# Expert outputs stored one row per slot and summed at the end; all token rows gathered by DMA

## The chip, the cores and the metric

The kernel runs on one core of a Trainium2 chip. The metric is the time of one execution on the device in microseconds (us), the median of several runs. All data are float32; "f32r" in tile types is float32 in the form that TensorE takes at its faster rate.

## The reference

Two encoder layers work on 512 tokens of width 1024. Each layer has a token mixer (attention and spatial gating) and then a mixture of experts, and it is the second half that is changed:

```python
scores = jax.nn.sigmoid((xt @ router_w).astype(jnp.float32))
...                                   # group-limited choice of 8 of 64 experts per token
wts = wts / jnp.sum(wts, -1, keepdims=True) * ROUTED_SCALE
...
def run_block(args):
    e, toks, ws = args
    xb = x_pad[toks]
    hb = jax.nn.silu(xb @ w_gate[e]) * (xb @ w_up[e])
    return (hb @ w_down[e]) * ws[:, None]
...
routed = jax.ops.segment_sum(yb.reshape(P, D), tok_buf, num_segments=T + 1)[:T]
shared = (jax.nn.silu(xt @ ws_gate) * (xt @ ws_up)) @ ws_down
return (routed + shared).reshape(B, S, D)
...
x = layer_norm(ALPHA * x + gate2 * y, ln2_g[l], ln2_b[l])
```

So 512 x 8 = 4096 rows of expert output have to reach 512 rows of the result. Each expert has 3 MB of weights (gate, up, down), 64 experts per layer.

## The kernel before

The experts are ranked by their number of tokens, and rank r has a fixed capacity `CAPS[r]`; the capacities add up to 43 **units** of 128 slots per layer (`UNITS`), each of one expert or of parts of two to four. A loop over an overflow count (L1141) takes what does not fit. The loop over `u_` (L1231) runs one unit after another: `gate_up` (L768), `turn` (L781), `down` (L793), with `swiglu` and the transposed copy between them on ACT and DVE. Weights come on SyncE's queue through rings: `we` (gate and up halves, 6 buffers, and 2 more as `w2`) and `wd` (3 buffers); a load waits until its buffer is free, and SP issues in program order.

**Inputs of a unit.** Units go in pairs. `mark_pair` (DVE, L1018) writes a one-hot matrix P of token by slot. For most pairs, `gather` on TensorE multiplies P with the token rows, split in two parts `xH` and `xL` (L1034, L1035: 64 matmuls a pair), into PSUM, and ACT and DVE write the modulated `xg` (L1040, L1042). For 8 of the 22 pairs of a layer (`by_dma`: even pairs 4 to 18), `bring_pair` fetches the rows from a copy of x in DRAM (`xd`) by two indirect DMAs of GpSimd (L1116) one pair ahead, and TensorE only transposes them (L1031, 16 per pair). `slots` (L1049) gives each slot's weight and token index by matmuls with P; GpSimd copies the indices of a unit's later segments to partition 0 (L1075).

**Outputs of a unit.** `down` leaves 128 rows `y` on DVE (L800), times weight and gate. `scatter` (L1084) adds them to a DRAM buffer by indirect DMAs with an add in the DMA, one for each segment of the unit, in turn on two buffers `accd[0]` and `accd[1]`; empty slots go to dump rows. The buffers are cleared first, and the shared expert's rows are written to `accd[0]` (L809 to L830). GpSimd also scales x and adds the bias during the first units (`stream`, L1169).

**The end of a layer.** Once unit 40 is scattered, `collect` loads the two buffers (8 loads of 512 KB, L1201) and GpSimd and DVE add them to x (L1207, L1208). The last two units (`LATE`) are not scattered: their rows are split and multiplied back by a one-hot `PT` on TensorE (L1297). Then each of the four tiles of 128 tokens is summed (L1302) and normalised, in the second layer scaled with `lnr` (loaded at L1278 and L1279, behind `collect` on SP's queue) and stored (L1285 to L1287). DVE, GpSimd and SP take their instructions in program order.

## Time and profile before

| | |
|---|---|
| median of 3 runs | 2220.01 us (2219.6 to 2223.42) |
| profiled execution | 2219.3 us, of which 2217.5 us are the span |
| TensorE (PE) busy | 2082.7 us, 94% of the span |
| DVE, ACT, GpSimd (POOL) busy | 1000.0, 518.9, 517.9 us |
| moved by DMA | 604.92 MB, mean 273 GB/s |
| mean granted TensorE clock | 0.985 |

"Span" is the time from the first to the last instruction; some 2 us lie around it. The busy share of PE is that of pipelined instructions that overlap, so 94% does not say that it works at its peak. "DMA share" in a stretch is the mean busy share of the 16 DMA engines; it reads 1.02 where they are never idle.

### The profile page before, as it was taken

How to read it: one execution, taken by the hardware profiler on the slowest of the kernel's cores; microseconds unless marked ns; L12 is line 12 of the kernel's file. 1: busy time of each engine (PE TensorE's matmuls, PEld its weight loads, DVE VectorE, ACT ScalarE, POOL GpSimd, SP SyncE). 2: the span in 40 equal slices, each digit the busy share in tenths (PEclk: the TensorE clock that was granted, in tenths of full speed). 3: DMA queues.
4: the chain of work that ended last, by engine and by line, in shares of the span. 5: the costliest groups of instructions: out<-in, count | busy, mean ns of one | idle time of the engine just before them, and what ended most of it. 6: DMA issues, size and time to landing. Idle time of an engine off the chain costs nothing. (4 is left out here: it accounts for less than half of the span.)

```text
span 2217.5 us, 31205 instructions
## 1 busy us (share of the span) xinstructions
PE 2082.7 (94%) x12088; PEld 1242.8 (56%) x12088; DVE 1000.0 (45%) x1920; ACT 518.9 (23%) x1005; POOL 517.9 (23%) x499
## 2 busy tenths in 40 slices
PE   5999999999999999999898999999999999999994
PEld 4888887464444444435477888855544435344442
DVE  6777866442222232222587675653422222222226
ACT  3463232211111111111144633222111111111111
POOL 3101002224222122212371000022522212222214
PEclk9999999999999999999999999999999999999997
DMA  7503755558999999999644045636799999999984
GB/s 271 187 29 126 243 211 191 232 201 300 383 382 384 392 383 385 382 384 348 221 140 139 11 150 163 205 114 247 275 328 380 385 390 383 381 363 384 391 291 156
DMA packets 113495, 604.92 MB, mean 273 GB/s; under 512 B 13984, under 2 KB 13984, under 8 KB 63424
## 3 DMA queue, kind: packets, MB, share of 16 engines
q1 hardware_dynamic: 90608, 525.82, 60.5%
q0 software_dynamic: 22736, 77.07, 14.1%
q8 instruction: 97, 1.59, 0.3%
q14 instruction: 54, 0.44, 0.1%
HBM read 542.54 MB, written 60.29 MB: 272 GB/s over the span
## 5 line engine op out<-in xcount | busy, mean ns | idle before, releaser
L768 PE MATMUL ps<-we,xg 128*32 128x512 f32 (+2 forms) x3648 | 642.6, 596 | 14.5 <-DMA we<-in_w_exp 10.4
L768 PEld LDWEIGHTS ps<-we,xg 128*32 128x32 f32 (+2 forms) x3648 | 198.2, 123 | 354.9 <-issue 316.5
L793 PE MATMUL ps<-wd,hTt 128*32 128x512 f32 (+2 forms) x1888 | 363.1, 595 | 19.6 <-DMA wd<-in_w_exp 16.1
L775 DVE TENSOR_TENSOR h<-h,ps 128x256 f32<-128x256 f32 x94 | 39.6, 421 | 556.8 <-ACT h L773 556.8
L1084 POOL DMA_INDIRECT accd<-y,ii x82 | 123.0, 1500 | 579.4 <-DVE y L800 476.4
L793 PEld LDWEIGHTS ps<-wd,hTt 128*32 128x32 f32 (+2 forms) x1888 | 118.5, 126 | 245.9 <-issue 195.7
L1034 PE MATMUL ps<-P,xH 128*128 128x256 f32 (+1 forms) x896 | 220.7, 286 | 6.0 <-DVE P L1018 6.0
L800 DVE SCALAR_TENSOR_TENSOR y<-ps,wc,r 128x512 f32<-128x512 f32 x172 | 128.9, 750 | 190.1 <-PE ps L793 190.1
L1035 PE MATMUL ps<-P,xL 128*128 128x256 f32 (+1 forms) x896 | 213.8, 282 | 0.0
L298 PE MATMUL ps<-wL,hH 128*128 128x512 f32 (+1 forms) x512 | 196.0, 383 | 7.3 <-DVE wL L294 7.3
L297 PE MATMUL ps<-wH,hH 128*128 128x512 f32 (+1 forms) x512 | 197.8, 386 | 4.2 <-ACT hH L193 4.2
L299 PE MATMUL ps<-wH,hL 128*128 128x512 f32 (+1 forms) x512 | 195.7, 382 | 0.0
L1034 PEld LDWEIGHTS ps<-P,xH 128*128 128x128 f32 x896 | 168.4, 188 | 19.3 <-issue 14.3
L1040 ACT ACTIVATE xg<-ps,f 128x256 f32<-128x256 f32 (+1 forms) x176 | 93.7, 559 | 356.9 <-DVE xg L1042 356.9
L1035 PEld LDWEIGHTS ps<-P,xL 128*128 128x128 f32 x896 | 168.5, 188 | 3.3 <-issue 3.3
L1042 DVE TENSOR_SCALAR xg<-ps,f 128x256 f32<-128x256 f32 (+1 forms) x176 | 90.5, 535 | 160.1 <-PE ps L1035 150.2
L193 ACT ACTIVATE hTt<-ps 128x256 f32<-128x256 f32 x94 | 36.1, 384 | 462.1 <-PE ps L781 462.1
L193 ACT ACTIVATE wH<-w 128x1024 fp32r<-128x1024 f32 x83 | 87.8, 1060 | 218.3 <-PE ps L299 129.5
L294 DVE TENSOR_TENSOR wL<-w,wH 128x1024 fp32r<-128x1024 f32 x84 | 109.9, 1310 | 54.2 <-ACT wH L193 54.0
L235 DVE SCALAR_TENSOR_TENSOR acc<-wa,cond,acc 128x1024 f32<-128x1024 f32 x80 | 117.1, 1464 | 12.8 <-issue 4.8
L298 PEld LDWEIGHTS ps<-wL,hH 128*128 128x128 f32 x512 | 98.8, 193 | 26.8 <-DVE wL L294 8.7
L297 PEld LDWEIGHTS ps<-wH,hH 128*128 128x128 f32 x512 | 98.5, 192 | 24.2 <-ACT hH L193 5.3
(326 smaller groups left out, 2566.3 us busy)
## 6 DMA issues: line engine op xcount, KB each, us to landing
we<-in_w_exp SPq DMA_DIRECT2D x256, 1024.0 KB, 16.7
wd<-in_w_exp SPq DMA_DIRECT2D x128, 1024.0 KB, 16.1
wa<-in_w_ada SPq DMA_DIRECT2D x96, 512.0 KB, 4.4
w<-in_wA SPq DMA_DIRECT2D x92, 512.0 KB, 4.3
sums<-accd SPq DMA_DIRECT2D x16, 512.0 KB, 7.1
accd<-zero POOLq DMA_DIRECT2D x12, 512.0 KB, 6.5
we<-in_w_sh SPq DMA_DIRECT2D x4, 1024.0 KB, 9.1
xd<-x SPq DMA_DIRECT2D x8, 512.0 KB, 2.6
```

Source lines behind the costliest of these rows:

```text
L193: return act.activation(out, in_, AF.Copy)
L235: dve.scalar_tensor_tensor(acc, w, cond[:, k:k + 1], acc, op0=OP.mult, op1=OP.add)
L294: dve.tensor_sub(l_out, src, h_out.bitcast(F32))
L297: pe.matmul(ps, aH, wH, start=first, stop=False)
L298: pe.matmul(ps, aH, wL, start=False, stop=False)
L299: pe.matmul(ps, aL, wH, start=False, stop=last)
L768: pe.matmul(ps[c:c + m, :], xT[:, k, c:c + m], ws[s][:, kk * 512:(kk + 1) * 512], start=k == 0, stop=k == NK - 1)
L793: pe.matmul(ps[c:c + m, :], t[:, j, c:c + m], ws[s][:, j * 1024 + nh * 512:j * 1024 + (nh + 1) * 512], start=j == 0, stop=j == 1)
L800: dve.scalar_tensor_tensor(y[0:n, hs], ps[0:n], wcol[0:n], gate2[0:n, hs], op0=OP.mult, op1=OP.mult)
L1034: pe.matmul(o, xH[:, i, k * 128:(k + 1) * 128], P[:, i, 0:n], start=i == 0, stop=False)
L1035: pe.matmul(o, xL[:, i, k * 128:(k + 1) * 128], P[:, i, 0:n], start=False, stop=i == NT - 1)
L1084: gp.indirect_dma_start(out=accd[turn_of[0]], out_offset=IndirectOffsetOnAxis(ap=ii[0:n, 0:1], axis=0), in_=y[col:col + n, :], in_offset=N ...
```

## The change

- A DRAM buffer `ysl` per layer has one row for each token and choice, 4096 rows. `slots` also computes the place of each slot (token x 8 + the number of earlier ranks that the token chose, from a small matmul with `above`), and `scatter` writes all 128 rows of a unit by one indirect DMA without an add. Slots without a token get an index past the bound and are skipped, in the gathers too.
- `collect` reads the 4096 rows back, 16 loads of 1 MB through the rings of `we` and `w2`. Per tile of 128 tokens DVE adds the first four rows, and TensorE the other four through `ident`. Units 41 and 42 stay `LATE`; zeros are scattered to their places when their rows are brought.
- All 22 pairs are brought by DMA, two pairs ahead, into four row buffers `rowbuf`, and transposed. `xH`, `xL`, the one-hot gather and GpSimd's index copies are gone.
- The shared expert's rows stay in SBUF (`ysh`, written by DVE) and GpSimd adds them to x in `stream`; `accd`, its clearing and the dump rows are gone.

```diff
-    accd = [dram.tile([640, D], F32, name=f"accd{a}") for a in range(2)]
-    xd = dram.tile([640, D], F32, name="xd")
+    xd = dram.tile([T, D], F32, name="xd")
+
+    ysl = [dram.tile([T * TOP, D], F32, name=f"ysl{l}") for l in range(DEPTH)]
...
-        xH = bp.tile([128, NT, D], F32R, name="xH")
+        ysh = bp.tile([128, NT, D], F32, name="ysh")
...
-                    acopy(y[0:n, hs], ps[0:n])
-                    gp.tensor_tensor(y[0:n, hs], y[0:n, hs], gate2[0:n, hs], op=OP.mult)
+                    dve.tensor_tensor(y[0:n, hs], ps[0:n], gate2[0:n, hs], op=OP.mult)
...
-        zero = bp.tile([128, D], F32, tag="y", bufs=3, name="zero")
-        gp.memset(zero, 0.0)
-        if l == 0:
-            gp.dma_start(xd[512:640, :], zero)
-        gp.dma_start(accd[0][512:640, :], zero)
-        for i in range(NT + 1):
-            gp.dma_start(accd[1][i * 128:(i + 1) * 128, :], zero)
...
         def shared_down(i):
-            y = down(sh_h[i], SH, 128, None)
-            gp.dma_start(accd[0][i * 128:(i + 1) * 128, :], y)
+            down(sh_h[i], SH, 128, None, ysh[:, i])
 
...
+        t1 = kc[:, C_T1:C_T1 + 4]
+        dve.tensor_scalar(WT[:, :, 192], t1, float(T + 1), float(TOP), op0=OP.subtract, op1=OP.mult)
+        dve.tensor_scalar(WT[:, :, 193], t1, float(T + 1), None, op0=OP.subtract)
+        dve.tensor_copy(WT[:, :, 194:196], t1[:, :, None].to_broadcast([128, NT, 2]))
...
-        xL = bring.tile([128, NT, D], F32R, tag="L16", name="xL")
-        for i in range(NT):
-            dve.tensor_sub(xL[:, i], x[:, i], xH[:, i].bitcast(F32))
...
+        def gather(rows, xg):
+
+            for k2 in range(4):
+                ps = psum()
+                for kk in range(2):
+                    for b_, r in enumerate(rows):
+                        pe.transpose(ps[:, kk * 256 + b_ * 128:kk * 256 + (b_ + 1) * 128],
+                                     r[:, (k2 * 2 + kk) * 128:(k2 * 2 + kk + 1) * 128], ident)
...
+        def slots(P, base, segs, rank, row):
+
+            ps = psum()
+            for i in range(NT):
+                pe.matmul(ps[:, 0:196], P[:, i, base:base + 128], WT[:, i], start=i == 0, stop=i == NT - 1)
+            sl = bp.tile([128, 196], F32, tag="sl", bufs=2, name="sl")
+            acopy(sl, ps[:, 0:196])
+            it = bp.tile([128, 1], I32, tag="it", bufs=4, name="it")
+            dve.tensor_scalar(it, sl[:, 193:194], float(T), None, op0=OP.add)
+            gp.indirect_dma_start(out=row, out_offset=None, in_=xd, in_offset=IndirectOffsetOnAxis(ap=it[:, 0:1], axis=0),
+                                  bounds_check=T - 1, oob_is_err=False)
+            wc = bp.tile([128, 1], F32, tag="wc", bufs=10, name="wc")
+            ii = bp.tile([128, 1], I32, tag="ii", bufs=10, name="ii")
+            tk = bp.tile([128, 1], F32, tag="tk", bufs=10, name="tk")
+            for r, off, col, n in segs:
+                for c, m in [(col, n)] if col == 0 else _pieces(col, n):
+                    b = slice(c, c + m)
+                    hi, lo, j = (sl[b, ds(rank + a, 1)] if rank is not None else sl[b, a + r:a + r + 1]
+                                 for a in (0, 64, 128))
+                    dve.tensor_tensor(wc[b], hi, lo, op=OP.add)
+                    dve.scalar_tensor_tensor(ii[b], j, float(T * TOP), sl[b, 192:193], op0=OP.add, op1=OP.add)
+            dve.tensor_copy(tk, sl[:, 194:195])
+            return wc, ii, tk
+
+        def scatter(y, ii):
+            gp.indirect_dma_start(out=ysl[l], out_offset=IndirectOffsetOnAxis(ap=ii[:, 0:1], axis=0), in_=y,
+                                  in_offset=None, bounds_check=T * TOP - 1, oob_is_err=False)
+
...
+        def mark_pair(p):
+            if not units_of(p):
+                return
+            P = bp.tile([128, NT, 256], F32R, tag="P", bufs=2, name="P")
+            for b_, u_ in enumerate(units_of(p)):
+                onehot(UNITS[u_], P, b_ * 128, lambda r: PW[:, :, r:r + 1])
+            Pd[p] = P
+
+        def bring_pair(p):
+
+            if not units_of(p):
+                return
+            P = Pd.pop(p)
+            for b_, u_ in enumerate(units_of(p)):
+                G[u_] = slots(P, b_ * 128, UNITS[u_], None, rowbuf[:, p % 2 * 2 + b_])
+                if u_ >= n_units - LATE:
+                    zero = bp.tile([128, D], F32, tag="y", bufs=3, name="zero")
+                    gp.memset(zero, 0.0)
+                    scatter(zero, G[u_][1])
+
+        def turn_pair(p):
+            xg = bp.tile([128, NK, 256], F32, tag="xg", bufs=2, name="xg")
+            gather([rowbuf[:, p % 2 * 2 + b_] for b_ in range(len(units_of(p)))], xg)
+            for b_, u_ in enumerate(units_of(p)):
+                G[u_] = xg[:, :, b_ * 128:(b_ + 1) * 128], *G[u_]
+
+        H = {}
+        mark_pair(0)
+        rowbuf = bring.tile([128, 4, D], F32, tag="L16", name="rowbuf")
+        bring_pair(0)
+        mark_pair(1)
+        bring_pair(1)
         shared_down(2)
         shared_turn(3)
...
 
 
...
                 gp.tensor_tensor(x[:, i], x[:, i], lnr[:, 1], op=OP.add)
                 yield
+                gp.tensor_tensor(x[:, i], x[:, i], ysh[:, i], op=OP.add)
+                yield
...
         def collect():
 
-            sums = []
             for i in range(NT):
-                t = bring.tile([128, 2, D], F32, tag="w", bufs=6, name="sums")
-                for a in range(2):
-                    nc.sync.dma_start(t[:, a], accd[a][i * 128:(i + 1) * 128, :])
-                sums.append(t)
-            for i, eng in ((0, gp), (2, gp), (1, dve), (3, dve)):
-                if eng is dve:
-                    yield
-                t = sums[i]
-                eng.tensor_tensor(t[:, 0], t[:, 0], t[:, 1], op=OP.add)
-                eng.tensor_tensor(x[:, i], x[:, i], t[:, 0], op=OP.add)
-            yield
...
+                for a in range(TOP // 2):
+                    t = wnew(0).rearrange("p (j d) -> p j d", j=2)
+                    src = ysl[l].rearrange("(t j) d -> t j d", j=TOP)
+                    nc.sync.dma_start(t, src[i * 128:(i + 1) * 128, 2 * a:2 * a + 2, :])
+                    got.append(t)
+
+        got = []
         for u_ in range(n_units + 1):
             if u_ % 2:
-                for p in (u_ // 2 + 2, u_ // 2 + 3):
-                    if by_dma(p) == (p == u_ // 2 + 3):
-                        mark_pair(p)
-            elif u_:
-                next_pair(u_ // 2 + 1)
-                if by_dma(u_ // 2 + 2):
-                    bring_pair(u_ // 2 + 2)
+                mark_pair(u_ // 2 + 3)
+            else:
+                if u_:
+                    turn_pair(u_ // 2 + 1) if units_of(u_ // 2 + 1) else None
+                bring_pair(u_ // 2 + 2)
...
-                slots_pair(*pair0)
-                next_pair(1)
+                turn_pair(1)
...
                 if u_ - 1 < n_units - LATE:
-                    scatter(y, UNITS[u_ - 1], idx)
+                    scatter(y, idx)
...
+                    collect()
                 drain(slow, 3)
...
+            mine = got[i * TOP // 2:(i + 1) * TOP // 2]
+            fin = [psum() for _ in range(2)]
...
-                                  start=own and n == 0 and a == 0, stop=n == LATE - 1 and a == 1)
-            if own:
-                for h in range(2):
-                    hs = slice(h * 512, (h + 1) * 512)
-                    dve.tensor_tensor(x[:, i, hs], fin[i, h], x[:, i, hs], op=OP.add)
-            normalise(x[:, i], [x[:, i, h * 512:(h + 1) * 512] if own else fin[i, h] for h in range(2)], 1e-5, True, both=i == NT - 1)
+                        pe.matmul(fin[h], PT[:, i * 128:(i + 1) * 128], yg[:, a, h * 512:(h + 1) * 512],
+                                  start=n == 0 and a == 0, stop=False)
+            for t in mine[:2]:
+                for j in range(2):
+                    dve.tensor_tensor(x[:, i], x[:, i], t[:, j], op=OP.add)
+            for n, t in enumerate(mine[2:]):
+                for j in range(2):
+                    for h in range(2):
+                        pe.matmul(fin[h], ident, t[:, j, h * 512:(h + 1) * 512], start=False, stop=n == 1 and j == 1)
```

## Rows read from the trace of the kernel before

**Rows 1.** Stretches of 40 us, first layer: span, PE, PEld, DVE, ACT, POOL, clock, DMA.

```profile
440.00:480.00 40.00, 37.07 (x218) 25.87 (x219) 11.88 (x35) 6.58 (x15) 1.03 (x4) 1.00 0.42 149
...
560.00:600.00 40.00, 40.00 (x216) 21.20 (x213) 11.90 (x33) 6.86 (x17) 7.92 (x11) 1.00 1.02 384
...
1040.00:1080.00 40.00, 40.00 (x181) 21.13 (x174) 8.26 (x18) 4.51 (x12) 7.05 (x5) 1.00 0.84 288
```

**Rows 2.** The DMA view, 450 to 1090 us: packets, MB, engine share; issues, us to landing.

```profile
q1 hardware_dynamic: 27643, 197.13, 75.3%
q0 software_dynamic: 8704, 29.89, 20.4%
...
sums<-accd SPq DMA_DIRECT2D x8, 512.0 KB, 7.3
accd<-y,ii POOLq DMA_INDIRECT x41, 9.3
...
xr<-xd,ii POOLq DMA_INDIRECT x16, 8.7
```

**Rows 3.** PE's timeline around the start of the first layer's loop.

```profile
440.79 0.36 PE L1034 MATMUL ps<-P,xH 128*128 128x256 f32 x1 [3.02 <-DVE P L1018]
...
448.42 0.28 PE L1035 MATMUL ps<-P,xL 128*128 128x256 f32 x1
450.83 7.13 PE L768 MATMUL ps<-we,xg 128*128 128x512 f32 x16 [2.14 <-SPq L753]
```

**Rows 4.** POOL's timeline: the last scatter of the first layer.

```profile
1071.23 1.56 POOL L1084 DMA_INDIRECT accd<-y,ii  x1 [7.61 <-DVE y L800]
```

**Rows 5.** The chain that ended last, 1836 to 1862 us: start, us, what.

```profile
1836.41 1.74 PE ps L1049 x16
1838.15 3.48 PE ps L768 x8
...
1860.14 1.86 PE ps L1031 x15
```

**Rows 6.** The DMA view of 450 to 520 us.

```profile
q0 software_dynamic: 441, 1.57, 11.9%
...
accd<-y,ii POOLq DMA_INDIRECT x3, 11.1
```

**Rows 7.** The DMA view of 360 to 450 us.

```profile
q0 software_dynamic: 1872, 6.82, 20.6%
...
accd<-zero POOLq DMA_DIRECT2D x6, 512.0 KB, 7.7
```

**Rows 8.** POOL's timeline in a pair that is brought by DMA.

```profile
1652.30 1.57 POOL L1084 DMA_INDIRECT accd<-y,ii  x1 [7.40 <-DVE y L800]
1662.92 0.86 POOL L1075 COPY is<-ii 32x1 int32<-32x1 int32 x4 [9.05 <-DVE ii L1066]
1664.34 1.01 POOL L1116 DMA_INDIRECT xr<-xd,ii  x1 [0.56 <-POOL is L1075]
1672.92 0.18 POOL L1075 COPY is<-ii 64x1 int32<-64x1 int32 x1 [7.57 <-DMA xr<-xd,ii]
1673.62 0.99 POOL L1116 DMA_INDIRECT xr<-xd,ii  x1 [0.52 <-POOL is L1075]
```

**Rows 9.** DVE's timeline at the end of the first and of the second layer.

```profile
1110.37 0.55 DVE L323 TENSOR_SCALAR x<-x,bnmv 128x512 f32<-128x512 f32 x1 [0.94 <-POOL bnmv L221]
...
2179.07 1.22 DVE L1208 TENSOR_TENSOR x<-x,sums 128x1024 f32<-128x1024 f32 x1
...
2200.35 1.28 DVE L1302 TENSOR_TENSOR x<-ps,x 128x512 f32<-128x512 f32 x2
...
2202.93 0.21 DVE L314 BATCH_NORM_AGGREGATE bnmv<-bnst 128x2 f32<-128x12 f32 x1
```

**Rows 10.** SP's queue at the end of the second layer.

```profile
2161.36 11.68 SPq L1201 DMA_DIRECT2D sums<-accd  x8
2173.14 0.94 SPq L1278 DMA_DIRECT2D lnr<-in_ln_g  x1
```

More of the change, by code (lines that the diff above doesn't have):

```diff
@@ L950, in moe @@
         acopy(XT, px.rearrange("p (i t) -> p i t", i=NT))
+        maskT = small([64, T], "maskT", BF16)
+        dve.tensor_scalar(maskT, px[0:64, :], 0.5, None, op0=OP.is_gt)
+        pe.matmul(pr[0:64, 128:192], kc[0:64, C_U:C_U + 64], perm[0:64, 0:64], start=True, stop=True)
+        above = small([64, E], "above", BF16)
+        dve.tensor_copy(above, pr[0:64, 128:192])
         shared_up(2, 0)
         shared_turn(1)
+        pj = psum()
+        for i in range(NT):
+            pe.matmul(pj[:, i * E:(i + 1) * E], maskT[:, i * 128:(i + 1) * 128], above, start=True, stop=True)
         pP = psum()
@@ L993, in moe @@
         shared_up(3, 1)
-        xL = bring.tile([128, NT, D], F32R, tag="L16", name="xL")
-        for i in range(NT):
-            dve.tensor_sub(xL[:, i], x[:, i], xH[:, i].bitcast(F32))
+        pe.matmul(po[0:1, 128:256], ones[0:64, 0:1], le, start=True, stop=True)
+        pe.matmul(po[:, 256:384], capb, lt, start=True, stop=True)
+        ovr = small([1, 132], "ovr", I32, keep=True)
+        dve.tensor_scalar(ovr[:, 0:128], po[0:1, 128:256], 63.0, None, op0=OP.min)
+        dve.tensor_copy(ovr[:, 128:129], po[0:1, 1:2])
@@ new lines, in gather @@
+        def gather(rows, xg):
[5 more added lines that the diff above has]
+                                     r[:, (k2 * 2 + kk) * 128:(k2 * 2 + kk + 1) * 128], ident)
+                n = 128 * len(rows)
+                for kk in range(2):
+                    k = k2 * 2 + kk
+                    o = ps[:, kk * 256:kk * 256 + n]
+                    if kk:
+                        act.activation(xg[:, k, 0:n], o, AF.Identity, bias=sh2[:, k:k + 1], scale=sc2[:, k:k + 1])
+                    else:
+                        dve.tensor_scalar(xg[:, k, 0:n], o, sc2[:, k:k + 1], sh2[:, k:k + 1], op0=OP.mult,
+                                          op1=OP.add)
@@ L1119, in gather_pair @@
-        def gather_pair(p):
-            if p not in Pd:
-                return None
-            P, n, us = Pd.pop(p)
-            xg = bp.tile([128, NK, 256], F32, tag="xg", bufs=2, name="xg")
-            gather(P, n, xg)
-            return P, us, xg
-        def slots_pair(P, us, xg):
-            for b_, u_ in enumerate(us):
-                wc, idx, _ = slots(P, b_ * 128, UNITS[u_], None, u_ >= n_units - LATE)
-                G[u_] = xg[:, :, b_ * 128:(b_ + 1) * 128], wc, idx
-        H = {}
@@ L1154, in moe @@
             onehot(segs, P, 0, lambda r: cur[:, :, None])
+            wc, idx, _ = slots(P, 0, segs, rv, rowbuf[:, 0])
             xg = bp.tile([128, NK, 256], F32, tag="xg", bufs=2, name="xg")
-            gather(P, 128, xg)
-            wc, idx, _ = slots(P, 0, segs, rv)
+            gather([rowbuf[:, 0]], xg)
             ps = psum()
@@ L1162, in moe @@
             y = down(t, segs, 128, wc)
-            scatter(y, segs, idx)
-        mark_pair(1)
+            scatter(y, idx)
+        mark_pair(2)
         more += [0, ch]
@@ L1279, in moe @@
             nc.sync.dma_start(lnr[:, 1], A["ln2_b"][l:l + 1, :].to_broadcast([128, D]))
-        for i in range(PRE):
-            begin(i)
         def affine(i):
@@ L1289, in moe @@
         for i in range(NT):
-            own = (i, 0) not in fin
-            if own:
-                for h in range(2):
-                    fin[i, h] = psum()
+            mine = got[i * TOP // 2:(i + 1) * TOP // 2]
+            fin = [psum() for _ in range(2)]
             for n, (PT, yg) in enumerate(lates):
```

163 lines of the change are left out of this document (35 added, 128 removed).

## Prediction

> **What bounds the kernel now.** I began with the table of 40 slices: PE is at 9 tenths nearly everywhere, but the DMA engines too are full from about 560 us to the end of each expert loop, so the share of busy PE says little. The windows make that exact: at the start of the loop the DMA engines are busy 0.42 of the time, then 1.02 at 384 GB/s, and near its end 0.84 [rows 1]. The loop of the first layer begins with unit 0 at 450.8 and its last scatter, of unit 40, is issued at 1071.2: 620.4 us [rows 3, 4]. The second layer repeats it within 5 us.
>
> Two budgets fill that time. For TensorE, the chain shows a pair of units at its own pace: 21.99 us from one pair's first matmul to the next transposes, 0.87 for its two slot products (1.74 stand there for four), and 1.86 to transpose a pair's rows [rows 5]. A one-hot gather takes 7.63 us, first to last start [rows 3]. Unit 0 to unit 40 are 20.5 pairs: 451 + 18, with 13 gathers on PE (99) and 8 transposed pairs (15): 583 us. For the DMA engines, between 450 and 1090 us SP's queue takes 75.3% of 640 us, 482 us for 197.13 MB, or 409 GB/s; without the 4.2 MB of `sums` the weights are 192.9 MB and 472 us. GpSimd's queue takes 20.4%, 130.6 us for 29.89 MB [rows 2]. With 2 us of instruction traffic that is 604 us of DMA work, 592 at the 1.02 that a full stretch shows. So DMA leads by a little, PE is close behind, and 28 us of the loop are DMA idle time, mostly at its two ends. Relieving PE alone would give nearly nothing; what counts is the DMA sum.
>
> **The change, part by part.**
>
> *Scatter without add.* Where only accumulating scatters run, GpSimd's queue needs 11.9% of 70 us, 8.3 us, for 1.57 MB: 188 GB/s [rows 6]. A plain write from the same queue is in the stretch before the loop: 6.82 MB in 20.6% of 90 us, 18.5 us, or 368 GB/s [rows 7]. The loop scatters 41 units, 21.5 MB, 114 us of the 130.6. Afterwards only real rows move: 4096 rows of 4 KB, 16.8 MB, the late units' zeros included. No plain indirect write stands in the trace; its bounds are 41 us at the weights' 409 GB/s and 89 us at the accumulating price. I take the plain price, as the nearest in kind: 45.6 us.
>
> *Gathers.* The 16 gathers of now are 8.4 MB. What is left of the 130.6 us for them is 16 us, and at 409 GB/s they would be 20.5. Afterwards all units are fetched; those of the first two pairs before the loop, so the loop has 39/43 of 16.8 MB, 15.2 MB: 29 to 41 us by those two rates and the plain 368. I take 37.
>
> *Sum of the loop.* DMA: 472 + 46 + 37 + 2 = 556 us, 545 at 1.02. PE: 20.5 x (21.99 + 0.87 + 1.86) = 507 us. PE falls by 76 us but DMA, which leads, only by 47; `collect` is outside both sums. The idle time of DMA should shrink, because PE no longer spends 7.63 us on each of the first pairs while the rings are full; 8 to 28 us, I take 20. Loop: 565, a gain of 55 us per layer (47 to 67 from the idle time alone).
>
> *Start of the loop.* The gather of pair 0 (7.6 us on PE) [rows 3] and the splitting of x go; in their place PE waits for one-hots of two pairs, and for gathers that land in some 8.7 us [rows 2], under 7 us of shared-expert matmuls. Between 8 us gained and 8 lost; I take nothing.
>
> *Edits costed at nothing.* The shared rows move from ACT and GpSimd to DVE, the slot indices from GpSimd to DVE, and `stream` gets four more additions on GpSimd: DVE and GpSimd are busy a third and a quarter of a loop window [rows 1]. Without that cover each addition on GpSimd would be some 2.4 us, twice DVE's 1.22 [rows 9]. The DMAs that cleared `accd` and stored the shared rows ran before the loop, while the DMA engines had room.
>
> *End of the first layer.* Now `collect` moves 4.2 MB and x is normalised 39.7 us after the last scatter (1110.37 + 0.55 - 1071.23) [rows 4, 9]. Afterwards 16.8 MB follow the last scatter: some 6 us until that scatter has landed (7.7 is the median of the plain ones) [rows 7], 41 us at 409 GB/s, 1 us more; then for the last rows 4 matmuls (1.7, at 3.48 for eight) [rows 5], 2.6 for two sums and statistics (2200.35 to 2202.93) [rows 9], and 2 for scale and store into x: 54 us, so 14 us are lost. Only four loads find buffers at once; the other buffers come free when units 41 and 42 are through and as DVE adds the first tiles, at 4 x 1.22 + 2.6 = 7.5 us a tile [rows 9] against 10.3 us of loading, so this should not stop the transfer.
>
> *End of the second layer.* The loads of `lnr` stand behind `collect` on SP: behind 8 loads they go out at 2173.1 [rows 10]; behind 16 that wait for buffers they land after the last of them, 50.5 us after the scatter. DVE needs them when it scales tile 0, which it does after it has normalised tile 1 and before it adds tile 2. So DVE stands until then, and two tiles of 7.5 us with two scalings of 1.5 (an estimate from the 1.22 us add, 1280 columns for 1024) come after: statistics end at 68.5, and the end is 14.6 later as now (2217.5 - 2202.9) [rows 9]: 83 us after the scatter against 56 (from 2161.4, where SP's first `sums` load follows it) [rows 10]. Loss 27; 10 if `lnr` came in time.
>
> **Sum.** 2219.3 - 2 x 55 + 14 + 27 = 2150. The median of the runs shown is 0.7 above the profiled execution: 2151 us.
>
> **Rivals.**
>
> *The gather chain takes over (slower, or a smaller gain).* In a pair that is brought by DMA, GpSimd issues a scatter at 1652.3; the next copies start 10.6 us later, the second gather's copy waits 7.57 us for the first gather's landing, and the second gather goes at 1673.6 and lands some 8.7 later: 30 us from the scatter to the rows [rows 2, 8]. The change gives a pair of gathers two units, 24.7 us of PE or 26.6 us of DMA. Against it: the copies go, so what makes the gathers wait for each other may go with them, and only a wait between scatters into the one `ysl` would stay. If the chain remains at 28 us a pair, the loop is 20.5 x 28 + 8 = 582 and the time 2184; at 30 us it is 623 and the time 2266. From 28.9 us a pair it is slower than before.
>
> *An indirect row costs what it costs now, with or without the add.* Then the scatters are 89 us: 600 of DMA, 588 + 20 = 608, time 2236. For it: all indirect writes of the trace accumulate, so that nothing shows the add alone. Against it: the gathers, which are indirect too, cost 16 to 20 us for 8.4 MB.
>
> *The empty slots are not skipped.* 22.5 MB of scatters (61 us) and 20.4 MB of gathers (50): 585, 573 + 20, time 2207.
>
> *Bytes and not engine time set the loop.* The loop moves 223.5 MB now, 360 GB/s over its 620 us; afterwards 192.9 + 16.8 + 15.2 = 224.9 MB, 625 us at the same rate, time 2270. Against it are 384 GB/s in a full stretch with accumulating scatters in it [rows 1], and their price of 188 [rows 6], which bytes alone don't explain. The Trainium skill ("DMA: Bandwidth & Descriptors", section "Where 436 GB/s comes from") says that for transfers between HBM and SBUF the HBM side binds at about 358 GB/s; by that the loop would be 628 us and the time 2276. The trace disagrees with that limit, with 384 GB/s over 40 us.
>
> **How the numbers follow.** The sum as it stands 0.57 (2120 to 2185, from the idle time, the start of the loop and the two ends); gather chain 0.20, half of it below 2215; price per row 0.08; no skipping 0.05; bytes 0.05; a better case, with idle time of 8 us and `lnr` in time, 0.05 (2105 to 2120). The predicted time is the likeliest case's. The range from 2110 to 2225 leaves out the upper half of the chain, the bytes, most of the price per row and a part of the best case, 0.2 together. A measurement of this kernel can tell about 0.2%, 4.4 us, from no change: faster 0.77, same 0.04, slower 0.19.
>
> **What would show it.** Right: no L1034 at all; GpSimd's queue at some 85 us per loop; a full DMA share from the first 50 us of the loop; a last scatter 565 us after unit 0; `collect` some 45 us long and DVE standing for `lnr` in the second layer only. Wrong: transposes that wait for row gathers in every pair (the chain), GpSimd's queue still above 120 us (price per row), a loop of full DMA engines at 360 GB/s (bytes), or loads of `collect` that wait long for buffers, which would make both ends worse.

## The result and the profile after

The changed kernel takes 2162.48 us (median of 4 runs, 2161.65 to 2163.16) against 2220.70 us for the kernel before, run beside it. The ratio is 0.9736, 95% interval 0.9719 to 0.9753: faster, by 58 us. The prediction was 2151 us, faster, with a range of 2110 to 2225. The profiled execution took 2163.16 us, with a span of 2160.9.

I read the new trace with the cuts that the prediction had made: where unit 0 starts, where the last scatter goes out, where x is normalised, and the end. First the two marks of the second layer before the change, PE's first matmul of unit 0 and the last scatter.

```profile
1536.18 7.13 PE L768 MATMUL ps<-we,xg 128*128 128x512 f32 x16 [2.02 <-SPq L753]
```

```profile
2160.94 1.56 POOL L1084 DMA_INDIRECT accd<-y,ii  x1 [7.61 <-DVE y L800]
```

Then the same marks after it: unit 0 in each layer (with the slot products of pair 2 ahead of it in the first), the last scatter of each layer, and the last row tile normalised in the first.

```profile
452.02 1.84 PE L1041 MATMUL ps<-WT,P 128*128 128x196 f32 x8 [3.87 <-DVE P L1015]
453.66 8.23 PE L770 MATMUL ps<-we,xg 128*128 128x512 f32 x16
```

```profile
1506.84 8.99 PE L770 MATMUL ps<-we,xg 128*128 128x512 f32 x16
```

```profile
1021.06 0.96 POOL L1062 DMA_INDIRECT ysl<-y,ii  x1 [9.70 <-DVE y L802]
```

```profile
2074.00 0.96 POOL L1062 DMA_INDIRECT ysl<-y,ii  x1 [9.70 <-DVE y L802]
```

```profile
1076.79 0.55 DVE L325 TENSOR_SCALAR x<-x,bnmv 128x512 f32<-128x512 f32 x1 [0.94 <-POOL bnmv L223]
```

With the first layer's marks from [rows 3, 4, 9] this splits the difference of the spans, 2217.5 to 2160.9, into six parts:

| part | before, us | after, us | difference | predicted |
|---|---|---|---|---|
| to unit 0, layer 1 | 450.8 | 453.7 | +2.8 | 0 |
| unit 0 to the last scatter | 620.4 | 567.4 | -53.0 | -55 |
| last scatter to x normalised | 39.7 | 56.3 | +16.6 | +14 |
| to unit 0, layer 2 | 425.3 | 429.5 | +4.2 | 0 |
| unit 0 to the last scatter | 624.8 | 567.2 | -57.6 | -55 |
| last scatter to the end | 56.6 | 86.9 | +30.3 | +27 |
| sum | 2217.5 | 2160.9 | -56.6 | -69 |

The two loops together were forecast to half a microsecond. Part of that is luck: the DMA work came out 5 us below the forecast and the idle time 7 above it, as the next rows show. The 12 us by which the time was too low lie at the two starts (7) and the two ends (6).

Next the first layer's loop in the new trace, from unit 0 to the last scatter: the windows view (span, busy time of PE, PEld, DVE, ACT and GpSimd, clock, DMA share, GB/s), and the DMA view of the same stretch (packets, MB, share of the engines).

```profile
453.66:1021.06 567.40, 540.67 (x3266) 211.74 (x3266) 166.49 (x497) 80.67 (x205) 120.22 (x96) 0.99 0.97 395
```

```profile
DMA packets 38120, 224.21 MB, mean 395 GB/s; under 512 B 6968, under 2 KB 6968, under 8 KB 14592
...
q1 hardware_dynamic: 26415, 192.42, 82.7%
q0 software_dynamic: 11664, 31.24, 14.1%
```

A share times 567.4 us is DMA work: SP's queue 469 us for the weights, as before; GpSimd's queue 80.0 us for 31.24 MB, where the prediction had 46 + 37 = 83. With 2 us of instruction traffic that is 551 us, 540 at the share of 1.02 that a full stretch shows [rows 1], and the other 27 us of the loop are DMA idle time; the prediction had 545 + 20. What PE waited for in this loop (us in total, times, longest):

```profile
PE ps L770 <- DMA we<-in_w_exp: 13.4, 12, 2.4
PE ps L796 <- DMA wd<-in_w_exp: 10.8, 8, 2.3
PE ps L1025 <- DMA rowbuf<-xd,it: 2.2, 1, 2.2
```

PE stands for weights, 24 us in all, and for a gather just once, 2.2 us. The chain of gathers that had a chance of 0.20 is not there. Two of the places where the DMA share falls, with a full stretch before them for comparison:

```profile
480.00:510.00 30.00, 27.85 (x155) 11.01 (x155) 10.39 (x35) 4.30 (x11) 23.62 (x13) 1.00 1.00 408
510.00:520.00 10.00, 10.00 (x64) 2.87 (x62) 3.19 (x6) 0.77 (x2) 9.13 (x6) 1.00 0.45 167
791.75:796.50 4.75, 3.46 (x30) 0.89 (x31) 0.93 (x2) 0.27 (x1) 0.00 (x0) 1.00 0.64 266
```

From 510 us the share falls to 0.45 while PE goes on, since for some 4 us nothing is moved at all. From 791.75 to 796.5 us it is 0.64 for another reason: counted in the trace, 10 to 14 packets are in flight there at every moment, mostly 10, all of them of SP's queue. So ten of the 16 engines still have weights to move while six have nothing. In SP's timeline two loads of down weights stand 18.78 us from 496.95 on and 14.97 us from 782.25 on, until PE frees their buffers, and whatever is behind them on SP waits too.

### The profile page after: what moved, and what is told of

Same layout as the page of the kernel before. It is cut to its first block, busy times and chain, and to the rows that moved or that the text cites. A ratio compares the mean times of both kernels' runs of the same rounds, so it can differ in the third digit from the quotient of the medians.

```text
span 2160.9 us, 29253 instructions
## 1 busy us (share of the span) xinstructions
PE 2005.1 (93%) x10868; PEld 1112.2 (51%) x10868; DVE 1006.4 (47%) x2142; ACT 495.3 (23%) x983; POOL 414.3 (19%) x366
## 5 line engine op out<-in xcount | busy, mean ns | idle before, releaser
L770 PE MATMUL ps<-we,xg 128*32 128x512 f32 (+2 forms) x3648 | 672.1, 601 | 29.2 <-DMA we<-in_w_exp 29.1
L770 PEld LDWEIGHTS ps<-we,xg 128*32 128x32 f32 (+2 forms) x3648 | 211.3, 124 | 386.1 <-issue 299.3
L796 PE MATMUL ps<-wd,hTt 128*32 128x512 f32 (+2 forms) x1888 | 374.6, 606 | 24.3 <-DMA wd<-in_w_exp 20.8
L796 PEld LDWEIGHTS ps<-wd,hTt 128*32 128x32 f32 (+2 forms) x1888 | 120.2, 127 | 255.3 <-issue 198.9
L1062 POOL DMA_INDIRECT ysl<-y,ii x82 | 87.6, 1069 | 789.6 <-DVE y L802 708.8
L1032 ACT ACTIVATE xg<-ps,f 128x256 f32<-128x256 f32 (+1 forms) x176 | 84.2, 557 | 210.1 <-DVE xg L1034 210.1
L1046 POOL DMA_INDIRECT rowbuf<-xd,it x86 | 87.8, 1021 | 227.4 <-DVE it L1045 184.5
L237 DVE SCALAR_TENSOR_TENSOR acc<-wa,cond,acc 128x1024 f32<-128x1024 f32 x80 | 116.9, 1461 | 13.3 <-DMA acc<-in_b_ada 8.9
L775 ACT ACTIVATE h<-ps 128x256 f32<-128x256 f32 x94 | 36.1, 384 | 346.6 <-PE ps L770 346.6
L301 PEld LDWEIGHTS ps<-wH,hL 128*128 128x128 f32 x512 | 98.3, 192 | 19.7 <-DVE hL L296 1.9
L1025 PEld LDWEIGHTS ps<-kc,rowbuf 128*128 128x128 f32 x688 | 75.9, 141 | 33.7 <-PE ps L796 16.6
L1025 PE MATMUL ps<-kc,rowbuf 128*128 128x128 f32 x688 | 84.1, 275 | 2.7 <-DMA rowbuf<-xd,it 2.7
## 6 DMA issues: line engine op xcount, KB each, us to landing
wd<-in_w_exp SPq DMA_DIRECT2D x128, 1024.0 KB, 16.6
x<-in_x SPq DMA_DIRECT2D x4, 512.0 KB, 11.2
```

The lines of the kernel that those rows point to most:

```text
L237: dve.scalar_tensor_tensor(acc, w, cond[:, k:k + 1], acc, op0=OP.mult, op1=OP.add)
L301: pe.matmul(ps, aL, wH, start=False, stop=last)
L770: pe.matmul(ps[c:c + m, :], xT[:, k, c:c + m], ws[s][:, kk * 512:(kk + 1) * 512], start=k == 0, stop=k == NK - 1)
L796: pe.matmul(ps[c:c + m, :], t[:, j, c:c + m], ws[s][:, j * 1024 + nh * 512:j * 1024 + (nh + 1) * 512], start=j == 0, stop=j == 1)
L1025: pe.transpose(ps[:, kk * 256 + b_ * 128:kk * 256 + (b_ + 1) * 128], r[:, (k2 * 2 + kk) * 128:(k2 * 2 + kk + 1) * 128], ident)
L1046: gp.indirect_dma_start(out=row, out_offset=None, in_=xd, in_offset=IndirectOffsetOnAxis(ap=it[:, 0:1], axis=0), bounds_check=T - 1, oob_i ...
```

## The experiments

All twelve kernels were timed beside the kernel before. "Loop" is unit 0 to the last scatter, first and second layer; after the change it is 567.4 and 567.2 us.

### Which part gave the gain

**The add put back.**

```diff
+        zt = att.tile([128, D], F32, tag="T4", name="zt")
+        gp.memset(zt, 0.0)
+        for i in range(T * TOP // 128):
+            gp.dma_start(ysl[l][i * 128:(i + 1) * 128, :], zt)
...
-    in_offset=None, bounds_check=T * TOP - 1, oob_is_err=False)
+    in_offset=None, bounds_check=T * TOP - 1, oob_is_err=False, compute_op=OP.add)
```

> The changed kernel with its scatters adding again: ysl is set to zero in a stretch in which its DMA engines are idle (from 112 us, and the same in the second layer), and each row is then added to that zero; all else is as changed. Theory (DMA engines lead the loop, and the add is what made a scatter dear): 16.8 MB at 188 GB/s are 89 us where the plain scatters took some 44, so each loop goes from 567 to 611 us and the time to 2250 us, slower than the original's 2220. Rival (a row costs the same with or without the add, and the gain came from elsewhere): GpSimd's queue stays at 81 us per loop and the time at 2162 to 2167. Rival (PE or the chain of gathers sets the loop, the DMA time is cover): the queue grows but the time stays below 2180.

2251.14 us (2249.25 to 2253.34), ratio 1.0133, interval 1.0116 to 1.0150: slower than before the change. The loops take 611.3 and 612.0 us. Windows and queues of the first:

```profile
456.02:1067.30 611.28, 558.04 (x3276) 212.99 (x3276) 168.24 (x500) 81.07 (x206) 144.92 (x96) 0.98 0.97 368
```

```profile
q1 hardware_dynamic: 26492, 192.93, 77.2%
q0 software_dynamic: 11664, 31.25, 19.9%
```

GpSimd's queue goes from 80.0 to 0.199 x 611.3 = 121.6 us for the same bytes, and the loop grows by 43.9. The add is what made a scatter dear, and the whole of it shows in the loop. It is not that gathers come late behind slower scatters: PE waits for gathered rows 5 us in this loop and for weights 48.

```profile
PE ps L1029 <- DMA rowbuf<-xd,it: 5.0, 2, 2.6
```

**The add taken away alone.** In the kernel before, with PE's one-hot gathers and the padded rows kept; each token's row then holds the last expert that wrote it instead of the sum.

```diff
-    in_=y[col:col + n, :], in_offset=None, compute_op=OP.add)
+    in_=y[col:col + n, :], in_offset=None)
```

> The original kernel with one thing changed: its scatters write without adding, so that a token's row holds the last expert that wrote it and not the sum. All else stays, the gathers on PE and the padded rows too. Theory (two budgets close together): DMA work falls by some 56 us per loop (21.5 MB at 368 instead of 188 GB/s), but PE's 583 us then lead, so a loop takes 593 to 600 us instead of 620 to 625 and the time is 2165 to 2180. Rival (the DMA engines alone count): 55 us per loop, 2110. Rival (the add costs nothing): 2220.

2177.38 us (2176.44 to 2178.45), ratio 0.9798, interval 0.9781 to 0.9814. Loops 602.6 and 601.0 us. The first:

```profile
450.58:1053.18 602.60, 598.44 (x3921) 284.47 (x3922) 176.66 (x443) 85.48 (x210) 115.47 (x144) 1.00 0.92 369
```

```profile
q1 hardware_dynamic: 26370, 192.08, 78.7%
q0 software_dynamic: 8560, 29.37, 12.5%
```

GpSimd's queue falls to 75.3 us; in the kernel before, cut to the same marks, it has 20.6% of 620.4, 127.8 us (130.6 in the longer stretch of [rows 2]). That is 52 less where 56 were expected. But the loop gains only 18: PE is busy 598.4 of its 602.6 us and the DMA share is down to 0.92. PE leads here.

The two runs and the two kernels make a square, first layer's loop: add and PE gathers 620.4; add alone removed 602.6; PE gathers (and padded rows) alone removed 611.3; both 567.4. The parts give 18 and 9 alone and 53 together, since each relieves one of two budgets that stood close to each other. (The kernel with the add put back also gathers more rows by DMA and skips empty slots, so 611.3 is the nearest that was run to PE's gathers alone.)

**More work for PE.** Every transpose of a gathered row done twice.

```diff
-        pe.transpose(ps[:, kk * 256 + b_ * 128: ...
+        for _ in range(2):
+            pe.transpose(ps[:, kk * 256 + b_ * 128: ...
```

> The changed kernel with every transpose of a gathered row done twice on PE into the same place: 84 us more of PE work in all, some 38 in each loop, no more DMA. Theory (after the change DMA leads with 547 + 20 us, PE needs 507): PE's sum comes level with DMA's at 545, most of the work is hidden, a loop takes 0 to 12 us more, time 2164 to 2187. Rival (PE sets the loop after the change): 38 us more per loop, 2240.

2169.12 us (2168.10 to 2170.38), ratio 0.9760, interval 0.9744 to 0.9776: 7 us more than the changed kernel. Loops 569.1 and 570.0 us, 2 to 3 longer for 328 more transposes, 38 us at 1.86 for 16 [rows 5]; the first:

```profile
457.08:1026.22 569.14, 560.90 (x3594) 243.96 (x3594) 178.50 (x499) 87.39 (x205) 120.46 (x96) 1.00 0.97 394
```

After the change PE has room, and the DMA sum leads. PE's busy time in the loop is 540.7 us after the change and not the 507 of the prediction, but here it rises by only 20 for 38 us more of work: so part of the busy time is not work that PE needs, and how much it needs can't be read from it.

### The two ends

**lnr ahead of collect**, and from GpSimd's queue.

```diff
+    if last:
+        lnr = bp.tile([128, 2, D], F32, tag="wd", bufs=WD_BUFS, name="lnr")
+        gp.dma_start(lnr[:, 0], A["ln2_g"][l:l + 1, :].to_broadcast([128, D]))
+        gp.dma_start(lnr[:, 1], A["ln2_b"][l:l + 1, :].to_broadcast([128, D]))
     collect()
...
-    nc.sync.dma_start(lnr[:, 0], A["ln2_g"][l:l + 1, :].to_broadcast([128, D]))
-    nc.sync.dma_start(lnr[:, 1], A["ln2_b"][l:l + 1, :].to_broadcast([128, D]))
```

> The changed kernel with the two loads of lnr of the second layer's end issued from GpSimd's queue ahead of collect, and not from SP's behind it. Theory: DVE's 13.65 us wait for lnr goes, the end of the second layer takes what that of the first takes, 54.8 us to the last statistics plus 14.6, 69 to 71 instead of 86.9 us after the last scatter: 2145 to 2148 us. Rival (DVE would then wait for the last of collect's loads instead, and that sets the end): at most 5 us are gained, 2157 or more.

2148.77 us (2146.32 to 2151.15), ratio 0.9672, interval 0.9656 to 0.9688: 14 us are gained, the wait that goes, and not the 15 to 17 expected. The end takes 73.8 us (last scatter at 2071.59, span 2145.4). For the changed kernel, SP's queue, DVE and GpSimd at the end of the second layer:

```profile
2078.26 29.36 SPq L1184 DMA_DIRECT2D we<-ysl  x16
2107.67 0.42 SPq L1227 DMA_DIRECT2D lnr<-in_ln_g  x1
```

```profile
2100.61 4.95 DVE L1246 TENSOR_TENSOR x<-x,we 128x1024 f32<-128x1024 f32 x4
...
2123.08 0.83 DVE L1232 TENSOR_TENSOR x<-x,lnr 128x640 f32<-128x640 f32 x1 [13.65 <-DMA lnr<-in_ln_g]
2124.30 1.14 DVE L1233 TENSOR_TENSOR x<-x,lnr 128x640 f32<-128x640 f32 x1 [0.40 <-DMA lnr<-in_ln_b]
...
2135.52 6.35 DVE L1246 TENSOR_TENSOR x<-x,we 128x1024 f32<-128x1024 f32 x4
```

```profile
2136.84 2.02 POOL L1232 TENSOR_TENSOR x<-x,lnr 128x384 f32<-128x384 f32 x1
2138.93 1.85 POOL L1233 TENSOR_TENSOR x<-x,lnr 128x384 f32<-128x384 f32 x1
```

The loads of lnr go out at 2107.7, behind 29 us of collect's, and DVE stands 13.65 us for them. DVE's four adds of a tile take 4.95 us at 2100.6, but 6.35 at 2135.5 while GpSimd scales its share of the tile before. With lnr early the same is left; DVE, and then PE's last tile:

```profile
2107.24 0.78 DVE L1232 TENSOR_TENSOR x<-x,lnr 128x640 f32<-128x640 f32 x1
...
2108.79 6.35 DVE L1246 TENSOR_TENSOR x<-x,we 128x1024 f32<-128x1024 f32 x4
...
2119.51 6.36 DVE L1246 TENSOR_TENSOR x<-x,we 128x1024 f32<-128x1024 f32 x4
...
2128.55 0.21 DVE L316 BATCH_NORM_AGGREGATE bnmv<-bnst 128x2 f32<-128x12 f32 x1
```

```profile
2118.36 7.13 PE L1250 MATMUL ps<-we,kc 128*128 128x512 f32 x16 [1.38 <-DMA we<-ysl]
```

The wait is gone, but the adds of the last two tiles take 6.35 us each, and with the scaling a tile needs 10.7 us of DVE: 2107.24 to 2117.96, and again to 2128.55. That now sets this end, though by little: PE's products of the last tile, which start 1.38 us late for the last load, end at 2125.5, 0.4 us before DVE has added its part. The Trainium skill ("SBUF — State Buffer", section "SBUF: two separate sides") says that a DVE operation with two inputs in SBUF and a GpSimd operation that reads SBUF exclude each other for a whole instruction. The trace agrees, with 6.35 against 4.95 us: in the chain of this run the two adds that fall on GpSimd's two scalings take 1.92 us each, the two before them 1.15 and 1.24.

**Half of collect's bytes.** Half of the sum's terms are left out, the work of DVE and PE is kept.

```diff
-    nc.sync.dma_start(t, src[i * 128:(i + 1) * 128, 2 * a:2 * a + 2, :])
+    nc.sync.dma_start(t[:, 0], src[i * 128:(i + 1) * 128, 2 * a, :])
...
-    dve.tensor_tensor(x[:, i], x[:, i], t[:, j], op=OP.add)
+    dve.tensor_tensor(x[:, i], x[:, i], t[:, 0], op=OP.add)
...
-    pe.matmul(fin[h], ident, t[:, j, h * 512: ...
+    pe.matmul(fin[h], ident, t[:, 0, h * 512: ...
```

> The changed kernel with collect reading every second row only, 8.4 MB instead of 16.8, each row then added twice: half of the sum's terms are left out, the work of DVE and PE is the same. Theory of the prediction (the bytes of collect set the ends): each end is 15 to 20 us shorter, 2120 to 2130. Rival (PE's own work sets the end just as much: from the last unit on it stands nowhere long, four tiles of 2.43 + 7.03 us): the first layer's end is at most 3 us shorter, the second's by the 14 us in which DVE waits for lnr, 2144 to 2149.

2150.22 us (2149.00 to 2153.49), ratio 0.9673, interval 0.9653 to 0.9694. The first layer's end takes 54.5 us instead of 56.3 (last scatter 1021.78, x normalised 1076.28); the second's 77.2 instead of 86.9, since lnr comes earlier. My theory of the ends falls. In the changed kernel's first end, SP's loads and PE (L1242 adds the late units, L1250 the rows), and then PE and the window of the run with half the bytes:

```profile
1026.32 28.36 SPq L1184 DMA_DIRECT2D we<-ysl  x16
```

```profile
1035.43 1.72 PE L1242 MATMUL ps<-yg,PT 128*128 128x512 f32 x5
...
1038.56 7.03 PE L1250 MATMUL ps<-we,kc 128*128 128x512 f32 x16
1045.03 2.43 PE L1242 MATMUL ps<-yg,PT 128*128 128x512 f32 x8
1047.29 7.03 PE L1250 MATMUL ps<-we,kc 128*128 128x512 f32 x16
...
1066.45 7.13 PE L1250 MATMUL ps<-we,kc 128*128 128x512 f32 x16 [0.86 <-DMA we<-ysl]
```

```profile
1039.29 7.03 PE L1250 MATMUL ps<-we,kc 128*128 128x512 f32 x16
...
1065.49 7.03 PE L1250 MATMUL ps<-we,kc 128*128 128x512 f32 x16
```

```profile
1021.78:1076.28 54.50, 50.80 (x148) 25.75 (x146) 37.97 (x54) 8.12 (x13) 12.59 (x14) 1.00 0.59 214
```

PE takes 8.73 us a tile (1047.29 less 1038.56) and can begin only when the last unit is through, 14 us after the last scatter; the loads take 10.3 us a tile but begin at 1026.3, 9 us earlier. So the two end together. With half the bytes, and a DMA share of 0.59, PE keeps its pace and only its waits of 0.4 and 0.9 us for the last loads go. Bytes and sums are level here, and halving the bytes alone gives 1.8 us. No run took away PE's sums alone; that this would give as little is not shown.

### The start

**One-hots of pair 2 ahead of the overflow loop, its gathers behind the first half of unit 0.**

```diff
+        mark_pair(2)
         with tc.For_i(0, nov, 1) as j:
...
-        mark_pair(2)
...
+            if u_ == 0:
+                bring_pair(2)
```

> The changed kernel with the one-hots of pair 2 marked ahead of the overflow loop, and the slot products and gathers of pair 2 issued behind the first half of unit 0's gate matmuls instead of ahead of them. Theory (while the rings are full the DMA engines wait for PE, so that a stall of PE ahead of unit 0 moves the whole loop): the 3.9 us that PE waits for those one-hots go in each layer, 2153 to 2159. Rival (the transfers of the loop end when they end, an earlier start of PE only makes it wait longer): the same within 2 us, 2160 to 2164.

2159.66 us (2156.47 to 2162.28), ratio 0.9713, interval 0.9690 to 0.9735, which overlaps that of the changed kernel. In the trace:

```profile
452.44 5.40 PE L770 MATMUL ps<-we,xg 128*128 128x512 f32 x8 [3.16 <-SPq L755]
```

The 3.87 us for the one-hots are gone, but PE now waits 3.16 us for SP (L755); unit 0 starts 1.2 us sooner, and the last scatter of the first layer goes out at 1022.5, not before 1021.1. A wait that stood behind another took its place. The median lies 3 us below the changed kernel's, between the ranges of the theory and of the rival, and the loop ends no earlier: no gain that these runs can tell.

**Both repairs** together (the two edits above):

> The changed kernel with both repairs, lnr from GpSimd's queue ahead of collect and the start of the loop as in the run that changes the start alone. The two are at different places, so their gains should add: 2148.8 less what the start alone gives, 2140 to 2147 if that is 2 to 9 us.

2145.68 us (2144.12 to 2149.58), ratio 0.9646, interval 0.9627 to 0.9665. It lies in the range expected, but the intervals of this run and of lnr alone overlap, and the loop's end (1022.67) hasn't moved, so I don't credit the start with it.

### What a skipped row saves, and where DMA idle time goes

**Empty slots moved.** They fetch the last token's row and write behind the real ones.

```diff
-    ysl = [dram.tile([T * TOP, D], F32, name=f"ysl{l}") for l in range(DEPTH)]
+    ysl = [dram.tile([T * TOP + 768, D], F32, name=f"ysl{l}") for l in range(DEPTH)]
...
-    dve.tensor_scalar(it, sl[:, 193:194], float(T), None, op0=OP.add)
+    dve.tensor_scalar(it, sl[:, 193:194], float(T), float(T - 1), op0=OP.add, op1=OP.min)
...
+    dve.scalar_tensor_tensor(fi[:, 1:2], sl[:, 192:193], 0.0, kc[:, C_DUMP:C_DUMP + 1], op0=OP.is_equal,
+                             op1=OP.mult)
+    dve.tensor_tensor(ii, fi[:, 0:1], fi[:, 1:2], op=OP.add)
...
-    in_offset=None, bounds_check=T * TOP - 1, oob_is_err=False)
+    in_offset=None, bounds_check=T * TOP + 767, oob_is_err=False)
```

> The changed kernel without the skipping: an empty slot fetches the last token's row and writes its result into a row of its own behind the real ones. Theory (a skipped row costs the DMA engines nothing): 5.7 MB more of scatters and some 3.5 MB more of gathers per loop at the prices of the changed kernel, 14 + 8 us, so GpSimd's queue goes from 81 to 103 us per loop, each loop is 20 to 24 us longer and the time is 2200 to 2212 us. Rival (a skipped row is paid like a moved one): queue at 81 us, 2160 to 2166.

2189.57 us (2187.99 to 2191.04), ratio 0.9846, interval 0.9826 to 0.9866: skipping is worth 27 us, not 38 to 50. The first loop:

```profile
455.32:1036.84 581.52, 544.80 (x3269) 212.03 (x3269) 178.70 (x578) 80.68 (x205) 120.30 (x97) 0.99 0.99 405
```

```profile
DMA packets 38141, 235.61 MB, mean 405 GB/s; under 512 B 4224, under 2 KB 4224, under 8 KB 14592
...
q1 hardware_dynamic: 26435, 192.58, 80.3%
q0 software_dynamic: 11664, 42.47, 18.4%
```

The packets of GpSimd's queue are as many as before, 11,664; 2,744 of those under 512 B have become full rows. The queue needs 0.184 x 581.5 = 107.0 us, 27 more for 11.2 MB (I had expected 22: gathers are 5.5 MB of it, not 3.5). But the loops grow by 14.1 and 13.3 only, and the DMA share rises to 0.99. Half of the work ran in time in which DMA engines had been idle.

**Four wd buffers.** On top of lnr ahead of collect.

```diff
-WD_BUFS = 3
+WD_BUFS = 4
-AHEAD = 8
+AHEAD = 7
...
-                if more[0] % (6 + MORE) >= 6:
+                if more[0] % (5 + MORE) >= 5:
...
-            return bring.tile([128, 2048], F32, tag="w", bufs=6, name="we")
+            return bring.tile([128, 2048], F32, tag="w", bufs=5, name="we")
```

> The kernel with lnr from GpSimd's queue, with four buffers for the down weights instead of three and five instead of six in the ring of the gate weights (and one load fewer ahead of the loop). Theory (the changed loop still has some 27 us of DMA idle time, part of it where SP's queue stands behind a wd load until PE frees one of three buffers, 15 us at 782 us): with a fourth buffer those dips go, a loop takes 5 to 10 us less, 2129 to 2139. Rival (the gate ring that is one shorter, and a later start, cost as much): 2145 to 2160.

2141.92 us (2139.14 to 2142.49), ratio 0.9640, interval 0.9620 to 0.9659: the fastest of all, but short of what was expected. Loops 563.9 and 564.5; with lnr alone, where nothing in the loop was changed, they are 568.7 and 564.3, so a loop is known to some 3 us. The first:

```profile
454.57:1018.42 563.85, 538.11 (x3266) 214.41 (x3266) 166.90 (x500) 80.50 (x205) 120.19 (x96) 0.99 0.98 400
```

SP's wait for PE's down matmuls (L796) falls from 241 to 63 us in this loop, and its wait for the gate matmuls (L770) rises from 40 to 184: the queue now stands for the shorter gate ring instead, and the DMA share is 0.98.

**The same with empty slots moved** (the edits of the run with empty slots moved and of the run with four wd buffers):

> The run before this one with the empty slots moved as well. In the changed kernel 27 us more of GpSimd's queue per loop made a loop only 14 us longer. Theory (the other half ran in the dips in which SP's queue stood behind wd): without the dips the whole shows, 24 to 27 us per loop, so 48 to 54 us more than the run with four wd buffers. Rival (it is hidden elsewhere): 26 to 32 us more, as in the changed kernel.

2169.99 us (2166.19 to 2172.87), ratio 0.9774, interval 0.9754 to 0.9794: 28 us more than the run before it, where my theory said 48 to 54. Loops 578.2 and 575.1, the first with a DMA share of 1.00:

```profile
455.21:1033.41 578.20, 543.76 (x3266) 211.88 (x3266) 178.71 (x578) 80.67 (x205) 120.07 (x96) 0.99 1.00 410
```

So the wd buffers are not where half of that work was hidden.

**Skipping undone for gathers alone** (of the edits for empty slots the one of `it`):

> The changed kernel with the skipping undone for the gathers alone: an empty slot fetches the last token's row, 5.4 MB more per loop, and scatters skip as changed. GpSimd's queue should go from 80 to some 93 us per loop. If each of these us shows, 2188; if half of them, as with gathers and scatters both, 2175; if gathers are hidden and the scatters are what counted, 2162 to 2168.

2169.73 us (2169.39 to 2172.37), ratio 0.9772, interval 0.9752 to 0.9792: 7 us more than the changed kernel. Loops 573.0 and 570.4, that is 5.6 and 3.3 more. The first:

```profile
q1 hardware_dynamic: 26420, 192.46, 81.6%
q0 software_dynamic: 11664, 36.75, 16.3%
```

GpSimd's queue takes 0.163 x 573.0 = 93.4 us for 36.75 MB, 13.4 more for 5.5 MB. Gathers hide more than half of their cost; the other 13.6 us of the run with all rows moved, the scatters', show some 9.

**Skipped rows added.**

```diff
+    xn = dram.tile([T, 64], F32, name="xn")
...
+            for _ in range(2):
+                no = bp.tile([128, 64], F32, tag="no", bufs=4, name="no")
+                gp.indirect_dma_start(out=no, out_offset=None, in_=xn, in_offset=IndirectOffsetOnAxis(ap=past[:, 0:1], axis=0),
+                                      bounds_check=T - 1, oob_is_err=False)
...
+        past = bp.tile([128, 1], I32, name="past")
+        dve.memset(past, T)
```

> The changed kernel with two more gathers behind each of its gathers, of 128 rows that are all out of bounds, so that every row is skipped and nothing is moved: 9,984 skipped rows more per loop, where the changed kernel has some 2,740. Moving those 2,740 rows cost 27 us more of GpSimd's queue but only 14 us of a loop. Theory A (a skipped row is not free: it holds a DMA engine for about half of what a moved one takes, without showing as busy; 13 us for 2,740): a loop is some 47 us longer and the DMA share falls, 2250. Theory B (a skipped row costs next to nothing, and the moved rows ran in idle time of the DMA engines while the rings were full): a loop is 0 to 6 us longer, mostly from GpSimd's own 2.6 us more per gather, 2162 to 2180.

2177.65 us (2175.93 to 2181.47), ratio 0.9795, interval 0.9779 to 0.9812. Loops 577.7 and 575.0: 10.3 and 7.8 more, neither the 47 of theory A nor the 0 to 6 of theory B. The first loop's packets say why it doesn't decide:

```profile
DMA packets 40667, 224.62 MB, mean 389 GB/s; under 512 B 9470, under 2 KB 9470, under 8 KB 17094
...
q0 software_dynamic: 14160, 31.29, 14.2%
```

78 gathers more have left 2,496 packets more, 32 each and not 128. Of the 32, 16 are those that every indirect DMA here has beside its 128 rows: the 81 of the changed loop (40 scatters, 39 gathers, two of zeros) have 144 each, which makes the 11,664. So 128 skipped rows of these gathers, 256 B long, left 16 packets, where a skipped 4 KB row leaves one of its own. The run doesn't price a skipped 4 KB row, and it also gave GpSimd 78 us more of work (198 us busy in the loop instead of 120).

## Why the prediction held, and where it was off

**The loop is led by the DMA sum, with PE close behind: right.** The kernel after and its variants show both sides. 42 us more of DMA work cost 44 us (add put back), 38 us more of PE work cost 2 to 3 (transposes twice), and without PE's relief 52 us less of DMA work gave 18 (add taken away alone). PE stood closer than the prediction had it: with the add alone away the loop takes 602.6 us, 598 of them with PE busy, where PE's sum was 583.

**Scatter without add: right, and somewhat too dear.** In the runs with empty slots moved, moving the skipped rows costs GpSimd's queue 13.6 us for 5.7 MB of scatters and 13.4 for 5.5 MB of gathers, 2.4 us a MB, which is what the weights pay (469 us for 192.4 MB). The single packets say the same: a 4 KB row takes 159 ns in the median, 327 ns where it is added (kernel before, add put back), and a skipped one 9 ns. I had taken the plain price, 2.7; the cheap bound was the true one. The rival that a row costs the same with or without the add is refuted by the run that puts it back. The Trainium skill ("Collectives: The Full Stack", section "Stop ④ — SDMA + CCE: where bytes move and the add happens") says of the adding transfers of a reduce-scatter that they are "read-read-write with the add free in between"; an estimate by that count of trips, three for two, would be 1.5 times a plain transfer. The trace disagrees with the estimate: 41.6 us on top of some 39 for 16.3 MB (36.75 MB less 39 gathers of 128 rows), 2.1 times.

**Idle time of the DMA engines: the level too low, the change right.** Between the same marks the kernel before has 75.5% of SP's queue and 20.6% of GpSimd's in 620.4 us, with instructions 598 us of work, 586 at 1.02 and 34 idle. Afterwards it is 551, 540 and 27. I had 604 and 28 before, 556 and 20 after: the stretch of [rows 2] is 20 us longer than the loop and caught some work of its ends. The difference, 7 us, is the 8 of the prediction; but what that time consists of was not in it (below).

**Start of the loop: 0 was forecast, it is 3 and 4 us.** The bound of 8 either way held. PE waits for the one-hots of three pairs (1.4, 1.9 and 3.9 us in the first layer) instead of running a gather, and the run on the start shows that a wait for SP stands close behind the last of them.

**Ends: right in size, wrong in one cause and one term.** 16.6 for 14, 30.3 for 27. The lnr wait is as described: the loads land 50 us after the last scatter, as worked out, and 14 us come back when they go out early. But "41 us at 409 GB/s" does not set the end of a layer alone; I had counted PE's identity matmuls for the last rows only, 1.7 us, while with the late units' they take 8.73 us of PE a tile, from a later start, and end level with the loading. And a tile of the second layer takes 10.7 us and not 9, since DVE's adds are slower beside GpSimd's.

**The bytes rival: refuted.** 395 GB/s over the whole loop, 405 and 410 with the empty slots moved, where 360 would have made it 625 us. The Trainium skill ("DMA: Bandwidth & Descriptors", section "Where 436 GB/s comes from") says that the HBM side binds transfers between HBM and SBUF at about 358 GB/s; the traces of this program on one core disagree, with those 395 to 410.

**Half of the cost of moving empty rows is hidden, though none of the add's was.** It isn't the wd buffers. A count of the packets in flight shows most of it: for 45 us of the changed kernel's first loop between 1 and 14 of the 16 DMA engines are at work, which loses 18 us of all 16; with the empty slots moved it is 15 us, and 7 lost. The same pair with four wd buffers has 41 and 15 us, the run with only the gathers moved 24. So with skipping some engines run out of work while others still have weights to move, as from 791.75 us on, and some 11 of the 13 hidden us went to such engines. What lies behind it is inferred, since no view names the engine of a row: that skipped rows are spread unevenly over the 16, and that the real rows, which the add makes dearer, lie on the engines that are behind as well.

**Left open:** whether a skipped 4 KB row holds a DMA engine for longer than its packet's 9 ns, since the run made for it turned out to have other packets. The edits that the prediction costed at nothing (rows and indices moved to DVE, additions in `stream`) were not priced one by one; with the loops as forecast they can't have cost much.

**A better version.** lnr ahead of collect and four wd buffers: 2141.92 us, ratio 0.9640 to the kernel before; 14 of the 21 us that it gains over the change come from lnr. The intervals of the two runs with and without the fourth buffer still touch, so the other 7 are not clear of noise.

## What to carry to other kernels

Make the sum of each budget for the stage and not for the kernel: where two stand within a few per cent, relieving one gives a fraction, and the pair of changes is worth more than its parts. A transfer moved behind a stage's end has to be followed to everything that queues behind it: here two small loads behind 16 large ones cost 14 of the 72 us that were to be had. Before calling an end bound by bytes, add up the work that the bytes feed; only halving one of the two tells. And a mean share of 16 DMA engines does not say whether all of them pause or some have run out of work.

## What the runs showed of the hardware

- An indirect write that adds costs about twice a plain one: 4.9 against 2.4 us a MB for 4 KB rows, 327 against 159 ns a row.
- A skipped 4 KB row still leaves a packet under 512 B, of 9 ns: the changed loop has 2,744 more of them than the loop with the empty slots moved (6,968 and 4,224), at equal totals. Each indirect DMA has 16 more small packets of its own. 128 skipped rows of 256 B left 16.
- Where rows are skipped, the 16 DMA engines run out of work at different times: in 45 of 567 us some but not all are at work, in 15 of 582 where nothing is skipped.
- DVE's four adds from SBUF take 6.35 us while GpSimd scales 128x384 elements twice, and 4.95 while it does not.
